# A hybrid encoder in f32: experts' steps in halves and in another order, gathers over expert 0's steps, attention scores in two row tiles

## Chip, cores and metric

One core of a Trainium2 chip. The metric is the device time of one execution, in microseconds; it is given as the median of some runs, and one further execution was recorded by the hardware profiler. Engines: PE is TensorE, PEld its weight loads, DVE VectorE, ACT ScalarE, POOL GpSimd, SP SyncE, which here only issues loads.

## What is computed

Two layers over 256 tokens of width 1024, all in f32. Cut to what matters here:

```python
for i in range(2):
    h = rms_norm(x, g_mix[i])
    q, k, v, u, gl = split(h @ w_in[i])          # q, k: 4 heads x 2 maps x 64; v: 4 heads x 128
    q, k = rope(q), rope(k)
    sc = einsum('bqhcd,bkhcd->bhcqk', q, k) * 64 ** -0.5
    pr = softmax(sc)
    a  = pr[:, :, 0] - lam * pr[:, :, 1]         # differential attention
    attn = rms_norm(einsum('bhqk,bkhe->bqhe', a, v), g_subln) @ w_attn_out[i]
    conv = silu(layer_norm(depthwise_conv(glu(u), width=31))) @ w_conv_out[i]
    x = x + (sigmoid(ga) * attn + sigmoid(gc) * conv) @ w_o[i]
    h = rms_norm(x, g_ffn[i])
    if i == 0: x = x + swiglu(h, w_ff_gu, w_ff_down)               # dense, 2816 wide
    else:      x = x + sum of the top 2 of 8 experts, each a swiglu 3584 wide
    x = x + sigmoid(rms_norm(x, g_ple[i]) @ w_ple_gate[i]) * (p[i] @ w_ple_proj[i])
return rms_norm(x, g_final)
```

An expert's weights are 1024 x 7168 and 3584 x 1024 in f32, 44 MB; the eight are 352 MB, and every one is loaded.

## The kernel before

**Dense part.** Both mixers, the dense feed-forward and the gates go through `panel` (matmuls at L298), whose weights ScalarE and VectorE first split into two parts (L272, L273). In the mixer, `scores(t)` makes for each of the 4 heads one product of 128 query tokens with both maps' 256 keys each (L426). So that one product of 128 rows makes both maps apart, the keys lie in `kTz` twice as wide: map 0's 64 rows with zeros under them, map 1's with zeros above, zeroed by POOL once per layer (L344, L345) and filled by two copies of ScalarE per 128 tokens (L409, L410). A product fills a PSUM bank of 512 columns; VectorE takes the negated maxima (L430), ScalarE the exponentials (L434). VectorE also runs most of the depthwise convolution into `acc` (L503), whose sums TensorE transposes (L191) behind the fourth gate panel. PE's order is the program's; that of the other engines is set by a scheduler.

**Experts.** The router ranks the experts by how many tokens chose them. Rank 0 is always expert 0; each rank has a fixed number of places for tokens, `SLOTS` = 64, 160, 96, 96, 96, 64, 32, 32, which is 2, 5, 3, 3, 3, 2, 1, 1 groups of 32. Tokens of a rank are gathered by a matmul (L988) into `first` (rank 0) or `xw`; `slot_scales` (L645) gathers their scales. Then an expert takes two chunks of its width, 2048 and 1536 columns of each half. For each chunk there are three steps: gate (8 loads of 1 or 0.75 MB), up (the same), down (8 or 6 loads of 1 MB). Every load is multiplied with each of the rank's groups in four column tiles of 32 (L848). After gate ScalarE applies silu out of PSUM (L874), after up VectorE multiplies (L880), before down TensorE transposes and ScalarE copies (L890, L891). After the last down step the result is scattered back to the token rows in four row tiles of 32 (L937) and added to `x` (L941); that is done in pieces beside the next expert's steps.

Two lanes, `b` with ranks 0, 6, 5, 7 and `a` with ranks 1, 2, 3, 4, are Python generators; each `next` on one writes out one step, and the loop at the end of `moe_main` decides which lane is next: `a` where the work written so far is at most `rate` times what was loaded. PE runs in that order. The gathers for ranks other than 0 are a third generator, `begin`, advanced twice after each step of expert 0; what is left of it runs before lane b's next expert.

The loads are issued by SP in the order in which TensorE uses them (`raw_block`, L255). The ring has twelve buffers of 1 MB (four `raw`, six borrowed from the dense part's weights, two in `raw2`); three more loads are made ahead into `early`. PSUM has eight banks of 512 columns for the expert part; a gate or up product takes one bank per group while it adds up, a down product one per two groups, and each bank of transposes, gather or scatter another.

Of the kernel before, what the change touches and what calls it, by code (L numbers as in the profile page):

```python
# [34 lines left out]
SLOTS = (64, 160, 96, 96, 96, 64, 32, 32)  # L35

# [14 lines left out]
def encoder_kernel(ctx: ExitStack, tc: tile.TileContext, A: dict, out: bass.AP):  # L51
# [270 lines left out]
    def mixer(i, nm, nxt, start=None, ready=(), between=None, last_hooks={}):  # L322
# [3 lines left out]
        with tc.tile_pool(name=f"mix{i}", bufs=1) as mp:  # L326
# [15 lines left out]
            with tc.tile_pool(name=f"att{i}", bufs=1) as ap, tc.tile_pool(name=f"attw{i}", bufs=2) as aw:  # L342
                kTz = ap.tile([P, NH, 2, SEQ], F32, name="kTz")
                nc.gpsimd.memset(kTz[64:128, :, 0, :], 0.0)  # L344
                nc.gpsimd.memset(kTz[0:64, :, 1, :], 0.0)  # L345
# [54 lines left out]
                def rope_T(qk):  # L400
                    for t in range(NT):
                        pt = trbank()
                        transposes([ras[qk, t][:, h * P:(h + 1) * P] for h in range(NH)], pt)
                        ptv = pt.rearrange("p (a b) -> p a b", a=NH)
                        ts = slice(t * P, (t + 1) * P)
                        if qk == 0:
                            nc.scalar.copy(qT[:, :, ts], ptv)
                        else:
                            nc.scalar.copy(kTz[0:64, :, 0, ts], ptv[0:64])  # L409
                            nc.scalar.copy(kTz[64:128, :, 1, ts], ptv[64:128])  # L410
# [12 lines left out]
                def scores(t):  # L423
                    for h in range(NH):
                        sc = bank()
                        nc.tensor.matmul(sc, qT[:, h, t * P:(t + 1) * P], kTz[:, h].rearrange("p c k -> p (c k)"),  # L426
                                         start=True, stop=True)
                        scv = sc.rearrange("p (c k) -> p c k", c=2)
                        mx = stat.tile([P, 2], F32, tag="nm", name="nm", bufs=4)
                        nc.vector.reduce_max(mx, scv, axis=AX.X, negate=True)  # L430
                        e = aw.tile([P, 2, SEQ], F32, tag="e", name="e")
                        se = stat.tile([P, 2], F32, tag="se", name="se", bufs=4)
                        for c in range(2):
                            nc.scalar.activation(e[:, c, :], scv[:, c, :], AF.Exp, bias=mx[:, c:c + 1],  # L434
# [378 lines left out]
    STEPS = [n for _, n in CHUNKS for _ in range(3)]  # L813
# [37 lines left out]
    def half_up(e, j, b):  # L851
# [4 lines left out]
        for k in range(KD):  # L856
            wt = made.pop(0) if made else raw_block(e.w_gu[:, k:k + 1, c0:c0 + n])
            e.product(ps, lambda i: e.xe[:, k, 32 * i:32 * i + 32], wt[:, 0], k == 0, k == KD - 1)
        return ps

    class Lane:


        def __init__(self, pool, name, groups):
            self.pool, self.name, self.groups = pool, name, groups
# [28 lines left out]
        def down(self, e, j, at):  # L894
# [9 lines left out]
            for l, (src, blocks) in enumerate(loads):  # L904
                wt = raw_block(src)
                for m, (g, f) in enumerate(blocks):
                    c = f * P + 32 * g
                    e.product(ps, lambda i: at[:, i, c:c + 32], wt[:, m], l + m == 0, l == len(loads) - 1 and m == 1)
            if j == 0:
# [9 lines left out]
        def scatter(self, e):  # L919
# [12 lines left out]
            for t in range(NT):  # L932
                po = [bank()[:, 0:256] for _ in range(4)]
                for i in range(e.groups):
                    for g in range(4):
                        rows = slice(32 * g, 32 * g + 32)
                        nc.tensor.matmul(po[g], selT[rows, i, t * P:(t + 1) * P], e.acc[rows, i, :], start=i == 0,  # L937
                                         stop=i == e.groups - 1, tile_position=(32 * g, 0))
                for g in range(4):
                    v = x[:, t, g * 256:(g + 1) * 256]  # L940
                    nc.vector.scalar_tensor_tensor(v, po[g], e.cmb[t], v, op0=ALU.mult, op1=ALU.add)  # L941
                yield

        def steps(self, experts, along):

# [6 lines left out]
            def beside():  # L952
                next(done, None)
                next(along, None)
                next(along, None)

            for n, make in enumerate(experts):
                if n == 1:
                    run(along)
                e = make()  # L960
                for j in range(len(CHUNKS)):
                    sil = self.silu(e, half_up(e, j, 0))
                    beside()
                    yield
                    self.times_up(e, half_up(e, j, 1), sil)
# [4 lines left out]
                    self.down(e, j, self.act_rows(e, j, sil))  # L970
# [288 lines left out]
```

## Time and profile before

| what | value |
|---|---|
| median of 3 runs | 1503.27 us (1502.98 to 1503.32) |
| the profiled execution: time, and span of its instructions | 1500.91 us, 1499.1 us |
| PE busy | 1419.3 us (95%) |
| DVE, ACT, POOL busy | 543.4, 435.1, 29.5 us |
| read from HBM | 455.41 MB, 304 GB/s over the span |
| costliest group | L848, gate and up matmuls: 453.1 us |

A busy PE is not PE at its peak: matmuls are pipelined, and ends are modelled. `A:B` in the rows is a stretch in us from the start of the span. In rows of groups the figures behind the first bar are busy time and mean ns of one, behind the second the idle time just before the group and what ended it. In rows in order of time the columns are start, length, engine, line and operation, with the idle time before in brackets. An f32 matmul of the program stands in the trace as two instructions.

### The profile page before, as it was taken

The page shows a single profiled execution, that of the slowest core. Times are in us where ns is not written, and L with a number is a line of the kernel's source. Part 1 is how long each engine was busy: PE and PEld are TensorE (multiplying, and loading weights), DVE is VectorE, ACT ScalarE, POOL GpSimd, SP SyncE. Part 2 cuts the span into 40 slices and gives each one's busy share as a digit, 9 for nine tenths or more (in the row PEclk, how much of TensorE's full clock was granted, in tenths as well). Part 3 has the DMA queues.
Part 4 walks back from the last instruction along what each step waited for, and adds up shares of the span by engine and source line. Part 5 has one row for each costly group of instructions (what it writes and reads, how often), then busy time and mean ns, then how long its engine had stood idle before and what let it go on. Part 6 is the DMA issues. An engine that isn't in the chain of part 4 may idle for free. (4 is left out here: it accounts for less than half of the span.)

```text
span 1499.1 us, 31163 instructions
## 1 busy us (share of the span) xinstructions
PE 1419.3 (95%) x13569; PEld 867.7 (58%) x13569; DVE 543.4 (36%) x1000; ACT 435.1 (29%) x748; POOL 29.5 (2%) x37
## 2 busy tenths in 40 slices
PE   8999999999999999999989999999999889899976
PEld 7777788888897777453436445244444244425346
DVE  5999665554779996100010000111010010001035
ACT  6595554443757854101000100000000000000005
POOL 2001000000000000000000000000000000000000
PEclk9999999999999999999999999999999899999998
DMA  9533655555545349897999999999999999999982
GB/s 314 186 113 113 205 183 180 186 171 177 197 168 169 111 146 370 325 368 289 407 378 419 390 397 416 421 419 419 416 417 419 421 419 418 418 419 417 410 338 85
DMA packets 116079, 458.55 MB, mean 306 GB/s; under 512 B 9590, under 2 KB 23360, under 8 KB 87264
## 3 DMA queue, kind: packets, MB, share of 16 engines
q1 hardware_dynamic: 114672, 454.69, 77.9%
q8 instruction: 108, 1.77, 0.5%
q10 hardware_dynamic: 1008, 1.65, 0.3%
q14 instruction: 35, 0.29, 0.1%
q0 software_dynamic: 256, 0.16, 0.0%
HBM read 455.41 MB, written 1.05 MB: 304 GB/s over the span
## 5 line engine op out<-in xcount | busy, mean ns | idle before, releaser
L848 PE MATMUL mm<-raw,xw 128*32 128x512 f32 (+1 forms) x4608 | 453.1, 549 | 23.5 <-DMA raw<-in_we_gu 23.4
L298 PE MATMUL mm<-w,hTb 128*128 128x512 f32 (+1 forms) x1632 | 335.3, 364 | 3.5 <-ACT hTb L218 2.9
L848 PEld LDWEIGHTS mm<-raw,xw 128*32 128x32 f32 x4608 | 149.8, 111 | 313.2 <-issue 243.0
L298 PEld LDWEIGHTS mm<-w,hTb 128*128 128x128 f32 x1632 | 275.7, 191 | 50.9 <-ACT hTb L218 3.3
L273 DVE TENSOR_TENSOR w<-raw,w 128x1024 fp32r<-128x1024 f32 (+1 forms) x196 | 228.8, 1178 | 131.5 <-ACT w L272 130.8
L848 PE MATMUL mm<-raw,aT 128*32 128x256 f32 x4480 | 248.8, 381 | 11.8 <-DMA raw<-in_we_down 8.3
L272 ACT CAST w<-raw 128x1024 fp32r<-128x1024 f32 (+1 forms) x196 | 197.8, 1017 | 207.0 <-PE mm L298 179.6
L848 PEld LDWEIGHTS mm<-raw,aT 128*32 128x32 f32 x4480 | 143.8, 110 | 111.4 <-DMA raw<-in_we_down 12.9
L880 DVE SCALAR_TENSOR_TENSOR s<-mm,rs,s 128x512 f32<-128x512 f32 (+1 forms) x40 | 27.4, 685 | 426.0 <-PE mm L848 363.3
L874 ACT ACTIVATE s<-mm,rs 128x512 f32<-128x512 f32 (+1 forms) x40 | 25.3, 634 | 333.5 <-PE mm L848 332.6
L891 ACT COPY aT<-mm 128x512 f32<-128x512 f32 (+1 forms) x40 | 19.2, 539 | 266.6 <-PE mm L890 266.5
L298 PE MATMUL mm<-w,hTa 128*128 128x512 f32 (+1 forms) x432 | 91.6, 369 | 3.4 <-DVE hTa L213 1.8
L503 DVE SCALAR_TENSOR_TENSOR acc<-zT,cw,acc 128x256 f32<-128x256 f32 x200 | 84.6, 479 | 0.1
L298 PEld LDWEIGHTS mm<-w,hTa 128*128 128x128 f32 x432 | 73.9, 188 | 18.2 <-DVE hTa L213 2.4
L298 PE MATMUL mm<-w,aTH 128*128 128x512 f32 x176 | 55.0, 391 | 0.0
L917 DVE TENSOR_TENSOR acc<-mm,acc 128x512 f32<-128x512 f32 (+1 forms) x13 | 7.0, 565 | 126.3 <-PE mm L848 126.3
L941 DVE SCALAR_TENSOR_TENSOR x<-mm,rcmb,x 128x256 f32<-128x256 f32 x64 | 26.2, 476 | 58.5 <-PE mm L937 58.5
L915 ACT COPY acc<-mm 128x512 f32<-128x512 f32 (+1 forms) x13 | 5.9, 489 | 141.2 <-PE mm L848 141.2
L185 POOL TENSOR_TENSOR rr<-rm,mhalf 128x2 f32<-128x2 f32 (+2 forms) x15 | 20.1, 1339 | 1248.2 <-DVE rm L183 1226.8
L930 DVE COPY aT<-mm 128x512 f32<-128x512 f32 (+1 forms) x13 | 7.4, 568 | 100.4 <-PE mm L191 100.4
L848 PE MATMUL mm<-raw,first 128*32 128x384 f32 (+1 forms) x464 | 43.7, 534 | 0.0
L298 PEld LDWEIGHTS mm<-w,aTH 128*128 128x128 f32 x176 | 33.0, 188 | 6.9
(239 smaller groups left out, 864.3 us busy)
## 6 DMA issues: line engine op xcount, KB each, us to landing
raw<-in_we_gu SPq DMA_DIRECT2D x125, 1024.0 KB, 19.8
raw<-in_we_down SPq DMA_DIRECT2D x112, 1024.0 KB, 19.4
raw<-in_we_gu SPq DMA_DIRECT2D x128, 768.0 KB, 14.9
raw<-in_w_in SPq DMA_DIRECT2D x35, 1024.0 KB, 4.9
raw<-in_w_ff_gu SPq DMA_DIRECT2D x22, 1024.0 KB, 5.0
raw<-in_w_ff_down SPq DMA_DIRECT2D x10, 1024.0 KB, 4.9
raw<-in_w_o SPq DMA_DIRECT2D x8, 1024.0 KB, 5.0
raw<-in_w_ple_gate SPq DMA_DIRECT2D x7, 1024.0 KB, 4.9
```

Of the source, the lines that this page charges most:

```text
L185: nc.gpsimd.tensor_tensor(r, m, mhalf[:, :count], op=ALU.pow)
L272: nc.scalar.copy(hi, src)
L273: nc.vector.tensor_tensor(lo, src, hi.bitcast(F32), op=ALU.subtract)
L298: nc.tensor.matmul(ps[t][:, :width], l, r, start=(k0 + k == 0 and j == 0), stop=(k0 + k == nk - 1 and j == 2))
L503: nc.vector.scalar_tensor_tensor(acc[:, c, :], zT[:, c, k:k + SEQ], wk[c], acc[:, c, :], op0=ALU.mult, op1=ALU.add)
L848: nc.tensor.matmul(ps[i][32 * g:32 * g + 32, :], a(i), w[:, g * q:(g + 1) * q], start=first and i % per == 0, stop=last and end, tile_posi ...
L874: nc.scalar.activation(s[:, i, 0:p.shape[1]], p, AF.Silu, scale=e.scale[:, i:i + 1])
L880: nc.vector.scalar_tensor_tensor(v, p, e.scale[:, i:i + 1], v, op0=ALU.mult, op1=ALU.mult)
L891: nc.scalar.copy(at[:, i, 0:n], pt[:, 0:n])
L917: nc.vector.tensor_tensor(d, p, d, op=ALU.add)
L930: nc.vector.tensor_copy(selT[:, i0:i0 + m, :], pt[:, 0:m * SEQ].rearrange("p (i c) -> p i c", i=m))
L941: nc.vector.scalar_tensor_tensor(v, po[g], e.cmb[t], v, op0=ALU.mult, op1=ALU.add)
```

## The change

- The scores: `kT` is as wide as `qT`, one copy per 128 tokens fills it, and there are no zeros. Two heads are taken together: four matmuls of 256 columns, each on 64 rows, write two banks, one per map, in two row tiles.
- An expert's step is divided: `half_up` and `down` yield in the middle of their loads, so a step is 4 loads (3 for the second chunk's down). The PSUM banks of a product stay taken through the yield.
- The order of the lanes follows a count, `waiting`, of loads that wait: 15 at first, and each step adds its loads times (0.36 x groups - 1), never below 0, with 0.8 more for each of the first 12 steps. Lane a is taken from step 6 on where the count after its step is at most 10. A lane that is about to begin a down product leaves the next step to the other.
- The gathers advance by one piece after each of the first half-steps, whichever lane it is.
- Lane b's scatter works with two banks at a time in place of four.

```diff
+GROUP, ROOM = 0.36, 10
@@ mixer
-                kTz = ap.tile([P, NH, 2, SEQ], F32, name="kTz")
-                nc.gpsimd.memset(kTz[64:128, :, 0, :], 0.0)
-                nc.gpsimd.memset(kTz[0:64, :, 1, :], 0.0)
+                kT = ap.tile([P, NH, SEQ], F32, name="kT")
...
-                            nc.scalar.copy(kTz[0:64, :, 0, ts], ptv[0:64])
-                            nc.scalar.copy(kTz[64:128, :, 1, ts], ptv[64:128])
+                        nc.scalar.copy((kT if qk else qT)[:, :, ts], ptv)
@@ scores
-                        nc.tensor.matmul(sc, qT[:, h, t * P:(t + 1) * P], kTz[:, h].rearrange("p c k -> p (c k)"),
-                                         start=True, stop=True)
+                        if h % 2 == 0:
+                            sc = [bank() for c in range(2)]
+                            for k in range(2):
+                                for c in range(2):
+                                    rows = slice(64 * c, 64 * c + 64)
+                                    nc.tensor.matmul(sc[c][:, k * SEQ:(k + 1) * SEQ], qT[rows, h + k, t * P:(t + 1) * P],
+                                                     kT[rows, h + k, :], start=True, stop=True, tile_position=(64 * c, 0))
...
@@ half_up, and the same in down
             e.product(ps, lambda i: e.xe[:, k, 32 * i:32 * i + 32], wt[:, 0], k == 0, k == KD - 1)
+            if k == KD // 2 - 1:
+                yield
@@ scatter
-                po = [bank()[:, 0:256] for _ in range(4)]
+                for g0 in range(0, 4, self.rows):
+                    gs = range(g0, g0 + self.rows)
+                    po = [bank()[:, 0:256] for g in gs]
@@ moe_main
-            todo = {k: [(n, n * SLOTS[i] // 32) for i in v for n in STEPS] for k, v in ranks.items()}
+            todo = {k: [(n / 2048 * 4, SLOTS[i] // 32) for i in v for n in STEPS] for k, v in ranks.items()}
+            steps, waiting, last, along = 0, 15.0, None, begin()
...
-                k = "a" if steps >= 3 and work <= rate * loaded else "b"
+                def after(k):
+                    n, groups = todo[k][0]
+                    return waiting + n * (GROUP * groups - 1)
+                k = "a" if todo["a"] and steps >= 6 and after("a") <= ROOM else "b"
...
+                waiting = max(0.0, after(k)) + (0.8 if steps < 12 else 0.0)
...
+                next(along, None)
+                if steps == 12:
+                    run(along)
```

PE, from expert 0's first down product to the first work of rank 1; `first` and `xw` are the gathered rows of expert 0 and of the others, `aT` the input of a down product, `x8` the number of matmuls. Before:

```order
L848 MATMUL mm<-raw,aT 32x256 x112
L848 MATMUL mm<-raw_5277,aT 32x256 x16
L988 MATMUL mm<-sel,ht 128x192 x32
L848 MATMUL mm<-raw,xw 32x512 x20
L848 MATMUL mm<-raw_5277,xw 32x512 x20
L848 MATMUL mm<-raw,xw 32x512 x120
L848 MATMUL mm<-raw,first 32x384 x24
```

PE, the first work of rank 1, now:

```order
L851 MATMUL mm<-raw,first 32x384 x16
L648 MATMUL mm<-tok_rstd,sel 32x1 x48
L851 MATMUL mm<-raw,xw 32x512 x80
L898 MATMUL mm<-ident,s 128x128 x6
L851 MATMUL mm<-raw,aT 32x256 x48
L851 MATMUL mm<-raw_5277,aT 32x256 x16
```

Rank 1's gate product stood behind expert 0's first chunk, 160 matmuls (8 loads) in a row; now it stands behind expert 0's second gate and up as well, 80 matmuls (4 loads), and expert 0's last down product follows before the other half.

PE, the scores of layer 0, between the value panel (`hTb`) and the transposes of the weights `a`. Before:

```order
L298 MATMUL mm<-w,hTb 128x512 x12
L426 MATMUL mm<-kTz,qT 128x512 x4
L298 MATMUL mm<-w,hTb 128x512 x48
L191 MATMUL tr<-ident,a 128x128 x8
L426 MATMUL mm<-kTz,qT 128x512 x4
```

The same place now:

```order
L300 MATMUL mm<-w,hTb 128x512 x12
L427 MATMUL mm<-kT,qT 128x256 x8
L300 MATMUL mm<-w,hTb 128x512 x48
L193 MATMUL tr<-ident,a 128x128 x8
L427 MATMUL mm<-kT,qT 128x256 x8
```

Nothing changed places; four matmuls of 512 columns became eight of 256.

PE, the end of the experts before, from the last gate and up loads of rank 4 (`xw`) on:

```order
L848 MATMUL mm<-raw,xw 32x384 x24
L890 MATMUL mm<-ident,s 128x128 x9
L848 MATMUL mm<-raw,aT 32x256 x72
L848 MATMUL mm<-raw_5277,aT 32x256 x24
...
L937 MATMUL mm<-acc,aT 128x256 x24
L890 MATMUL mm<-ident,s 128x128 x3
L848 MATMUL mm<-raw,aT 32x256 x48
L191 MATMUL mm<-ident,cols 128x128 x2
L937 MATMUL mm<-acc,aT 128x256 x8
```

The end now, from rank 4's last down loads on:

```order
L851 MATMUL mm<-raw,aT 32x256 x144
L193 MATMUL mm<-ident,cols 128x128 x6
L949 MATMUL mm<-acc,aT 128x256 x24
L851 MATMUL mm<-raw,xw 32x384 x4
...
L851 MATMUL mm<-raw,xw 32x384 x36
...
L898 MATMUL mm<-ident,s 128x128 x3
L851 MATMUL mm<-raw,aT 32x256 x48
L193 MATMUL mm<-ident,cols 128x128 x2
L949 MATMUL mm<-acc,aT 128x256 x8
```

Before, rank 7's gate and up had been done ahead of rank 4's last down product, and six down loads were left to it; now its whole second chunk, 22 loads, comes after rank 4 is done.

## Rows read from the trace of the kernel before

**Rows 1.** The page: GB/s of all loads in 40 equal slices of the span.

```profile
GB/s 314 186 113 113 205 183 180 186 171 177 197 168 169 111 146 370 325 368 289 407 378 419 390 397 416 421 419 419 416 417 419 421 419 418 418 419 417 410 338 85
```

**Rows 2.** Stretches: length, busy us of PE, PEld, DVE, ACT, POOL; clock, DMA share, GB/s.

```profile
600.00:620.00 20.00, 19.33 (x154) 8.01 (x155) 4.85 (x35) 2.86 (x4) 0.00 (x0) 0.85 0.64 241
660.00:700.00 40.00, 40.00 (x408) 13.00 (x401) 0.00 (x0) 3.44 (x5) 0.00 (x0) 1.00 0.70 248
740.00:780.00 40.00, 36.56 (x426) 14.77 (x418) 5.53 (x9) 1.55 (x3) 0.00 (x0) 1.00 0.95 370
840.00:880.00 40.00, 40.00 (x504) 16.13 (x498) 0.00 (x0) 3.49 (x6) 0.00 (x0) 1.00 0.97 377
1000.00:1020.00 20.00, 20.00 (x244) 7.77 (x240) 0.00 (x0) 0.59 (x1) 0.00 (x0) 1.00 1.01 418
```

**Rows 3.** PE in order of time, the first steps of the experts.

```profile
603.19 6.69 PE L848 MATMUL mm<-early,first 128*32 128x512 f32 x48 [0.67 <-ACT first L742]
...
618.39 2.03 PE L988 MATMUL mm<-sel,ht 128*128 128x192 f32 x16
...
636.18 1.09 PE L645 MATMUL mm<-tok_rstd,sel 128*32 128x1 f32 x96
...
638.63 14.11 PE L848 MATMUL mm<-raw,aT 128*32 128x256 f32 x256 [0.20 <-ACT aT L891]
...
656.41 34.54 PE L848 MATMUL mm<-raw,xw 128*32 128x512 f32 x320
690.77 10.50 PE L848 MATMUL mm<-raw,first 128*32 128x384 f32 x128
```

**Rows 4.** Waits of the SP queue, 660 to 700 us: in total, times, longest.

```profile
SPq L255 <- PE mm L848: 35.9, 14, 6.7
```

**Rows 5.** PE in order of time, where it waits for every load: 1 MB, then 0.75 MB.

```profile
953.99 1.92 PE L848 MATMUL mm<-raw,xw 128*32 128x512 f32 x16 [0.56 <-DMA raw<-in_we_gu]
956.49 1.92 PE L848 MATMUL mm<-raw,xw 128*32 128x512 f32 x16 [0.57 <-DMA raw<-in_we_gu]
...
1419.97 1.51 PE L848 MATMUL mm<-raw,xw 128*32 128x384 f32 x8 [0.55 <-DMA raw<-in_we_gu]
1421.85 1.51 PE L848 MATMUL mm<-raw,xw 128*32 128x384 f32 x8 [0.37 <-DMA raw<-in_we_gu]
```

**Rows 6.** Groups of the whole span: expert products, transposes, and what empties their banks.

```profile
L848 PE MATMUL mm<-raw,xw 128*32 128x512 f32 (+1 forms) x4608 | 453.1, 549 | 23.5 <-DMA raw<-in_we_gu 23.4
L848 PE MATMUL mm<-raw,aT 128*32 128x256 f32 x4480 | 248.8, 381 | 11.8 <-DMA raw<-in_we_down 8.3 <-ACT aT L891 3.5
L880 DVE SCALAR_TENSOR_TENSOR s<-mm,rs,s 128x512 f32<-128x512 f32 (+1 forms) x40 | 27.4, 685 | 426.0 <-PE mm L848 363.3 <-issue 61.1
L874 ACT ACTIVATE s<-mm,rs 128x512 f32<-128x512 f32 (+1 forms) x40 | 25.3, 634 | 333.5 <-PE mm L848 332.6
L890 PE MATMUL mm<-ident,s 128*128 128x128 f32 x140 | 21.7, 302 | 0.0
```

**Rows 7.** Groups of the whole span: scores, and the scatter in four row tiles.

```profile
L426 PE MATMUL mm<-kTz,qT 128*128 128x512 f32 x32 | 14.5, 597 | 0.0
L937 PE MATMUL mm<-acc,aT 32*128 32x256 f32 x320 | 21.1, 391 | 0.6 <-DVE aT L930 0.6
```

**Rows 8.** From the scores to the convolution's end: stretches, then PE's waits, both layers.

```profile
74.10:137.50 63.40, 58.95 (x267) 45.12 (x266) 59.80 (x134) 50.67 (x111) 5.43 (x2) 1.00 0.31 103
469.20:530.80 61.60, 58.65 (x267) 45.11 (x266) 59.13 (x132) 50.07 (x111) 3.74 (x2) 1.00 0.32 106
137.56 1.44 PE L191 MATMUL tr<-ident,acc 128*128 128x128 f32 x6 [2.44 <-DVE acc L503]
530.84 1.16 PE L191 MATMUL tr<-ident,acc 128*128 128x128 f32 x6 [1.67 <-DVE acc L503]
```

**Rows 9.** Near the experts' end: a stretch of PE, then PE's last product.

```profile
1418.00:1420.00 2.00, 1.38 (x12) 0.57 1.01 418
1453.90 1.07 PE L848 MATMUL mm<-raw,aT 128*32 128x256 f32 x16 [1.15 <-DMA raw<-in_we_down]
```

More of the change, by code (lines that the diff above doesn't have):

```diff
@@ L812, in encoder_kernel @@
     CHUNKS = ((0, 2048), (2048, 1536))
-    STEPS = [n for _, n in CHUNKS for _ in range(3)]
+    STEPS = [n for _, n in CHUNKS for _ in range(6)]
     made = []
@@ L858, in half_up, with __init__ @@
             e.product(ps, lambda i: e.xe[:, k, 32 * i:32 * i + 32], wt[:, 0], k == 0, k == KD - 1)
+            if k == KD // 2 - 1:
+                yield
         return ps
     class Lane:
-        def __init__(self, pool, name, groups):
-            self.pool, self.name, self.groups = pool, name, groups
+        def __init__(self, pool, name, groups, rows=4):
+            self.pool, self.name, self.groups, self.rows = pool, name, groups, rows
         def tile(self, kind, n=512):
@@ L908, in down @@
                     e.product(ps, lambda i: at[:, i, c:c + 32], wt[:, m], l + m == 0, l == len(loads) - 1 and m == 1)
+                if l == len(loads) // 2 - 1:
+                    yield
             if j == 0:
@@ L932, in scatter, with steps @@
             for t in range(NT):
-                po = [bank()[:, 0:256] for _ in range(4)]
[L934 to L941, printed above, removed]
+                for g0 in range(0, 4, self.rows):
+                    gs = range(g0, g0 + self.rows)
+                    po = [bank()[:, 0:256] for g in gs]
+                    for i in range(e.groups):
+                        for p, g in zip(po, gs):
+                            rows = slice(32 * g, 32 * g + 32)
+                            nc.tensor.matmul(p, selT[rows, i, t * P:(t + 1) * P], e.acc[rows, i, :], start=i == 0,
+                                             stop=i == e.groups - 1, tile_position=(32 * g, 0))
+                    for p, g in zip(po, gs):
+                        v = x[:, t, g * 256:(g + 1) * 256]
+                        nc.vector.scalar_tensor_tensor(v, p, e.cmb[t], v, op0=ALU.mult, op1=ALU.add)
                 yield
-        def steps(self, experts, along):
+        def steps(self, experts):
             done = iter(())
@@ L953, in beside @@
                 next(done, None)
[L954 to L959, printed above, removed]
+            for make in experts:
                 e = make()
                 for j in range(len(CHUNKS)):
-                    sil = self.silu(e, half_up(e, j, 0))
+                    sil = self.silu(e, (yield from half_up(e, j, 0)))
                     beside()
                     yield
-                    self.times_up(e, half_up(e, j, 1), sil)
+                    self.times_up(e, (yield from half_up(e, j, 1)), sil)
                     beside()
@@ L969, in steps @@
                         run(done)
-                    self.down(e, j, self.act_rows(e, j, sil))
+                    yield from self.down(e, j, self.act_rows(e, j, sil))
                     beside()
@@ L1107, in unit @@
                             [pc[:, t, 1:2] for t in range(NT)])
-                run(Lane(mp, "r", MORE // 32).steps([lambda: ex], iter(())))
+                run(Lane(mp, "r", MORE // 32).steps([lambda: ex]))
         def units(u):
```

26 lines of the change are left out of this document (10 added, 16 removed).

## The prediction

> **What bounds the kernel now.** I read the page first, its row of GB/s over 40 slices [rows 1]: up to about slice 14 the loads run far below what they reach later, so the dense part (both mixers, the dense feed-forward, the router) is TensorE's; from slice 24 to slice 37 they sit at 410 to 421 GB/s, so the experts, some 353 MB of weights in 368 loads, are bound by the loads there. In between, slices 15 to 23, most are short. Cut more finely, that stretch is where loads are lost [rows 2]: against the 418 GB/s of 1000 to 1020 us, the window at 600 us lacks 177 of 418 for 20 us, that is 8.5 us of loading; 660 to 700 lacks 170 for 40 us, 16.3 us; 740 to 780, 4.6 us; 840 to 880, 3.9 us. Together 33.3 us in which the load queue stood still for want of a free buffer.
>
> Why it stood still: twelve loads fit the ring, and a load is issued only when TensorE has finished with the one twelve before. The order of work on TensorE [rows 3] has a step of rank 1, which has five groups of 32 slots, from 656.41 for 34.54 us: 8 loads, 4.32 us each. A load of 1 MB takes 2.50 us and one of 0.75 MB 1.88 us where TensorE is waiting for them [rows 5]. So such a load adds 0.73 of a load to those that wait, eight of them 5.8. In those 40 us the SP queue waits 35.9 us for matmuls of L848 [rows 4]. TensorE in turn waits for loads 23.4 and 8.3 us in the whole expert part [rows 6], at other places: with few groups it is quicker than the loads. Both sides are idle by turns, which is what an order of work can mend; the bytes can't be.
>
> **Expert steps, first piece: the start.** The prices are: 34.54 us/(8 loads x 5 groups) = 0.864 us for one group of a 1 MB gate or up load; 10.50/(8 x 2) = 0.656 for a 0.75 MB one; 14.11/(8 x 2) = 0.882 for a down load [rows 3]. No arithmetic is added or removed. The first 8.5 us (600 to 620) stay: fifteen loads are in before TensorE begins at 603.19, three of them outside the ring, and nothing in the change begins earlier.
>
> Then expert 0 runs whole before rank 1, but for its last six loads, with the gathers between its half-steps. Its 40 loads cost 15.2 us for the first eight (603.19 to 618.39), 8 x 2 x 0.864 = 13.8, 14.1 for eight down loads, 16 x 2 x 0.656 = 21.0; three gathers of 2 x 2.03 + 1.09 make 15.5, and ten transposes [rows 6] 1.5: 81 us, to about 684. Loads restart near 613, so 71 us: nine of 1 MB (22.5), sixteen of 0.75 (30.1), and 18.5 us for 7.4 more. Fifteen and 32.4 have come, 40 are used: about 7 wait. The first piece of rank 1 now has 4 loads, +2.9: about 10 wait, at which point the other two are on their way. So of the 16.3 us nearly all goes; where the gathers fall late in expert 0 the ring is close to full, for which I leave 1.7 us (0 to 3).
>
> **Second piece: the middle.** Next come six loads of rank 0 and sixteen of rank 6 (one group, 0.864 us against 2.50): the ten that wait are used up, TensorE waits for loads near 725 us, and that costs nothing while the loads run. From there to the fourth half-step of rank 2 I add up: gate and up of 1 MB, 12 x 5 + 16 x 2 + 16 x 3 = 140 group-loads x 0.864 = 121 us; 0.75 MB, 16 x (5 + 1 + 2) = 128 x 0.656 = 84; down, 14 x (5 + 1 + 2) = 112 x 0.882 = 99; 56 transposes at 21.7/140 make 9 [rows 6]. Scatters of five groups are 5.3 us (21.1/20 each [rows 7]), and 4 us go to their selections and to lane b's scatter in two halves instead of four row tiles at once. That makes 322 us. The loads in it take 86 x 2.50 + 48 x 1.88 = 305 us. TensorE falls 17 us or 6.8 loads behind; the next three half-steps add 1.3. Ten may wait, so there is a margin of 1.9 loads, 5 us, and the two stalls of 4.6 and 3.9 us go too, unless something slows TensorE.
>
> That something has no row: a product cut in two keeps its PSUM banks through the other lane's step. Rank 1 holds five of eight, the other lane one or two, and the next product or transpose may wait until a bank is emptied. Emptying one takes 634 ns on ScalarE or 685 on VectorE [rows 6]. In the stretch 18 products begin. Bounds: no wait at all, or two evictions, 1.3 us, at each: 23 us, less the margin 18 us of lost loading. I take one of 0.634, 11.4 less 5: 6.4 us, since the order leaves another lane's half-step between most products and the next use of their banks.
>
> **Third piece: the end.** The last six half-steps are rank 7's alone: 22 loads with one group, bound by the loads, as the end is before. Of TensorE's clock the rows show that with 0.75 MB loads and little to do it had sunk to 0.57 of full at 1418 us, and eight instructions then take 1.51 us [rows 5, 9], where 0.656 is their full price. After the last load there are 1.07 us of matmuls [rows 9], a transpose and a scatter of about 1.2 us: at half clock at most 3 us more. I take 1.5. Once started, the part behind keeps its length.
>
> So the loads lose 8.5 + 1.7 + 6.4 = 16.6 us where they lost 33.3: 16.7 gained, less 1.5: **15.2 us**.
>
> **Scores.** Before, 16 products of 128x512 with half of the rows zero take TensorE 14.5 us [rows 7]. Now 32 of 128x256, each on half of the rows, two at a time. That row tiles do run side by side in this type is seen at L937, where 320 instructions of 391 ns each take 21.1 us, six at a time with the pipelining; those of L426 overlap 1.3 times. So 7.2 us of TensorE go, 3.6 in each layer. But VectorE has no room: from the scores to the end of the convolution it is busy 59.80 of 63.40 us in the first layer and 59.13 of 61.60 in the second [rows 8], and TensorE waits 2.44 and 1.67 us for the convolution's last sums even now. An earlier TensorE waits longer there. Only VectorE's own gaps can shrink, 3.6 + 2.5 = 6.1 us; the floor is 0, and I take the middle, **3 us**. ScalarE loses four copies and POOL four memsets, and neither is what ends last there. The maxima are as many as before, over as many elements.
>
> The Trainium skill's page "TensorEngine Tiling (Array Packing)", in Performance Considerations under PSUM Bottleneck, speaks against this edit: tiling speeds up TensorE but not the emptying of PSUM, which may then be the limit. The two VectorE rows agree that the limit is there. By that rule taken whole, this edit would give nothing, and the sum would be 1488 us.
>
> **Sum.** 15.2 + 3 = 18.2 us. The profiled execution, 1500.91 us outside of its span of 1499.1, would become 1482.7; the median of the runs is 2.4 us above the profiled one, so 1503.27 - 18.2 = **1485 us**.
>
> **Rivals.** *Banks make it slower.* If at each of the 35 half-steps of the middle TensorE waits two evictions, 46 us, less the margin 41, the loads lose 8.5 + 1.7 + 41 = 51 us against 33.3, and with the end and the scores the time is 1503.3 + 18 + 1.5 - 3 = 1520. It passes from gain to loss at 30 us of such waits, 0.85 us at each half-step. For it: five, two and one make eight banks. Against it: the two evicting engines are idle in nearly all of this part (VectorE 0.00 us busy from 660 to 700 [rows 2]), so a bank is emptied as soon as its product ends, and the scatter of lane b asks for two banks only. Chance 0.06.
>
> *The ring fills later instead.* The count starts from 15 waiting and adds for gathers; it runs rank 6 dry early, so that the heavy work is pushed behind 734 us. If TensorE's extra in the middle is 16 to 20 us and not 11.4, the stall returns near 1060 to 1100 us: 11 to 15 us lost there, 8.5 + 1.7 + 12, a gain of 11 - 1.5, and without the scores 1494 (1491 to 1500). Chance 0.18.
>
> *All of it comes.* No bank wait, no cold end, VectorE's gaps closed: 33.3 - 8.5 + 6.1 = 31 us, 1472; with some of it 1471 to 1478. Chance 0.10.
>
> *The change does nothing that counts.* The order by loads waiting moves the stalls without removing them, as the sum of work and the ring are the same: 1500 to 1506. Against it is the ledger of the start, which needs no unknown. Chance 0.06.
>
> **Numbers.** My forecast, 1478 to 1491, has 0.60. The range takes it in with about half of the better case and most of the one in which the ring fills later: 1475 to 1494. A measurement of this kernel tells 0.2%, 3 us, from no change. Faster 0.60 + 0.18 + 0.10 = 0.88, same 0.06, slower 0.06.
>
> **What would show it.** In the profile of the changed kernel: 605 to 613 us still empty of loads; 660 to 700 near 415 GB/s; TensorE waiting for loads of rank 6 near 725; the lowest later window between 1050 and 1110, at 330 GB/s or more over 40 us; the last 45 us with TensorE waiting at every load. The score products take some 7 to 8 us, and TensorE's waits for `acc` grow from 2.4 and 1.7 to 3 to 5. I am wrong if the first product of half-steps waits for ScalarE or VectorE by more than 25 us together, if windows from 740 to 1000 are short, or if the waits for `acc` do not grow.

## The result, and the profile after

The changed kernel takes 1489.62 us, the median of 6 runs (1484.58 to 1494.8), beside 1503.3 for the kernel before (1501.16 to 1507.19): the ratio, against the runs made beside it (median 1505.15), is 0.9897, 95% interval 0.9879 to 0.9914. That is 15.5 us faster (12.9 to 18.2), where 18.2 were forecast. The profiled execution took 1484.58 us with a span of 1482.8; before it was 1500.91 and 1499.1. Both lie at the fast end of their kernel's runs, 5.0 and 2.4 us under the medians.

The page's row of GB/s in 40 slices, which answers to [rows 1]:

```profile
GB/s 314 187 119 116 205 179 190 171 183 159 224 169 144 115 169 319 307 379 418 421 419 419 417 418 418 418 402 419 404 382 417 422 417 418 420 419 417 415 339 81
```

From slice 18 to 37 it stands at 415 to 422, but for slices 26, 28 and 29. Four stretches of the changed kernel, columns as in [rows 2]:

```profile
600.00:620.00 20.00, 19.32 (x148) 7.19 (x147) 3.89 (x31) 2.36 (x3) 0.00 (x0) 0.81 0.54 206
640.00:700.00 60.00, 59.57 (x902) 31.55 (x895) 2.04 (x6) 5.90 (x13) 0.00 (x0) 1.00 0.99 393
960.00:980.00 20.00, 20.00 (x323) 11.54 (x319) 0.00 (x0) 2.01 (x5) 0.00 (x0) 1.00 0.97 391
1060.00:1100.00 40.00, 40.00 (x646) 22.32 (x638) 2.83 (x7) 2.42 (x5) 0.00 (x0) 1.00 0.97 370
```

Reckoned as in the prediction, against 418 GB/s, they lose 10.1, 3.6, 1.3 and 4.6 us: 19.6 where 33.3 were lost. So 13.7 us of loading came back. The SP queue's waits from 1060 to 1100 us (in total, times, longest) show why 4.6 did not:

```profile
SPq L257 <- PE mm L851: 32.8, 18, 6.2
```

SP waits there for TensorE to free a buffer, as it did at 660 to 700 before [rows 4]. And TensorE does not wait for emptied banks. These are its waits from 738 to 1100 us:

```profile
PE mm L193 <- DVE cols L1014: 2.1, 2, 1.1
PE mm L851 <- ACT aT L899: 1.8, 4, 0.7
PE mm L851 <- DMA raw<-in_we_gu: 1.5, 2, 0.9
PE mm L949 <- DVE s L888: 0.2, 1, 0.2
```

No gate, up or down product waits for a bank. The waits for other engines are those for transposed activations, for the scatter's columns and 0.2 us of a scatter for a bank that VectorE empties: 4.1 us in 362.

At the scores, TensorE in order of time, layer 0:

```profile
74.26 2.00 PE L427 MATMUL mm<-kT,qT 64*128 64x256 f32 x16
...
109.20 1.12 PE L193 MATMUL tr<-ident,o 128*128 128x128 f32 x4 [2.42 <-ACT aT L452]
...
135.71 1.52 PE L193 MATMUL tr<-ident,acc 128*128 128x128 f32 x6 [2.49 <-DVE acc L506]
```

and the same place before:

```profile
74.12 3.67 PE L426 MATMUL mm<-kTz,qT 128*128 128x512 f32 x8
...
110.50 0.66 PE L191 MATMUL tr<-ident,o 128*128 128x128 f32 x4 [0.42 <-ACT aT L449]
```

A block of score products takes 2.00 us; before, the two blocks took 3.67 and 3.60. The wait for `acc` is what it was [rows 8]; new is 2.42 us at the transposes of `o`, for ScalarE's copy of `aT`. Before, that wait was 0.42.

### The profile page after: what moved, and what is told of

It reads as the page before. It is cut to its first block, busy times and chain, and to the rows that moved or that the text cites. A ratio compares the mean times of both kernels' runs of the same rounds, so it can differ in the third digit from the quotient of the medians.

```text
span 1482.8 us, 31201 instructions
## 1 busy us (share of the span) xinstructions
PE 1415.2 (95%) x13601; PEld 873.8 (59%) x13601; DVE 543.4 (37%) x1000; ACT 432.0 (29%) x744; POOL 23.2 (2%) x33
## 5 line engine op out<-in xcount | busy, mean ns | idle before, releaser
L851 PE MATMUL mm<-raw,xw 128*32 128x512 f32 (+1 forms) x4608 | 444.8, 543 | 16.3 <-DMA raw<-in_we_gu 16.3
L851 PE MATMUL mm<-raw,aT 128*32 128x256 f32 x4480 | 252.0, 384 | 6.8 <-ACT aT L899 3.5
L300 PEld LDWEIGHTS mm<-w,hTa 128*128 128x128 f32 x432 | 75.5, 191 | 18.2 <-DVE hTa L215 2.4
## 6 DMA issues: line engine op xcount, KB each, us to landing
raw<-in_we_gu SPq DMA_DIRECT2D x125, 1024.0 KB, 17.8
```

The lines of the kernel that those rows point to most:

```text
L300: nc.tensor.matmul(ps[t][:, :width], l, r, start=(k0 + k == 0 and j == 0), stop=(k0 + k == nk - 1 and j == 2))
L851: nc.tensor.matmul(ps[i][32 * g:32 * g + 32, :], a(i), w[:, g * q:(g + 1) * q], start=first and i % per == 0, stop=last and end, tile_posi ...
```

## Experiments

| kernel | median us | ratio to before, 95% interval |
|---|---|---|
| e1_scores: scores alone | 1505.07 | 0.9999 (0.9986 to 1.0012) |
| e2_experts: experts alone | 1490.74 | 0.9913 (0.9899 to 0.9927) |
| e3_again: the change | 1489.7 | 0.9893 (0.988 to 0.9907) |
| e4_price: other numbers in the count | 1482.07 | 0.9859 (0.984 to 0.9877) |
| e5_old_rule: halves, old order | 1501.72 | 0.9968 (0.9956 to 0.998) |
| e6_whole_steps: count, no halves | 1496.25 | 0.9927 (0.9908 to 0.9945) |
| e7_early_last | 1478.83 | 0.9822 (0.9802 to 0.9842) |
| e8_gathers_before | 1492.25 | 0.9887 (0.9856 to 0.9917) |
| e9_scores_kept_busy | 1502.94 | 0.9983 (0.9967 to 0.9999) |
| e10_best_kept_busy | 1480.45 | 0.9831 (0.9808 to 0.9855) |
| e11_early_again | 1477.15 | 0.9808 (0.9785 to 0.983) |
| e12_scores_own_bank | 1504.6 | 0.9997 (0.9984 to 1.001) |

Before was 1505.63 beside e1 to e4, 1506.12 beside e5 to e8, 1504.71 beside e9 to e11, 1505.64 beside e12.

### The two parts apart

**e1_scores** is the kernel before with only the `kT` and `scores` part of the diff; **e2_experts** is the changed kernel with the old `kTz` and `scores`.

> The kernel before with the scores in two row tiles, and nothing of the experts changed. Theory A (my forecast, the ledger of the dense part): the row tiles give 3 us of 1503.3, so 1500.3, ratio 0.998; at most 6.1, 1497.2. Theory B, from the profile of the changed kernel: the score products do take 2.00 us a block where they took 3.67, but the transposes of o now wait 2.42 us for ScalarE where they waited 0.42, and later stretches run at a lower granted clock (0.91 in 520 to 560 us), so that at the experts' start only 0.46 us of 2.9 were left: 1502.8, ratio 0.9997, same. Theory C: the lower clock comes from the scores' new wait, takes more than they give and makes the runs' times spread: 1503 to 1506, with runs more than 6 us apart. A profile in which the experts start at 600 us or earlier speaks for A, at 602.5 to 603.2 for B, later than 603.2 for C.

> The changed kernel with the mixers of the kernel before: the expert part alone. Theory A (ledger of loads): of 33.3 us that the load queue stood still, 13.7 come back and 1.4 us at the branch behind the experts, 15.1 in all: profiled 1485.8, median 1488.2, ratio 0.990. Adding e1's result gives the whole change to within 1.5 us. Theory B: the two parts help each other (an earlier start of the experts also fills the loads' ring): this one gains less than 12 us, over 1491. Theory C (the scores' new waits bring the lower clock and the spread of 10 us between the runs of the changed kernel): this one gains 17 to 18 us, 1485 to 1486, with runs within 5 us of each other.

The scores alone gain 0.2 us (-1.8 to 2.1): theory B's time, though the experts began at 605.62 us, theory C's sign; my 3 us fall. The experts alone gain 13.1 us (11.0 to 15.2), theory A, and their profiled execution was 1482.83. Runs of e2 lay 11 us apart (1482.83 to 1494.3), as far as those of the change, and those of the kernel before beside them 8 us, for 9 in e1, so the spread does not come from the scores: C falls there. The two do not quite add up: beside them the change gained 16.1 us (14.0 to 18.1, e3), 2.8 more than the two apart, where I had allowed 1.5. That is within the noise of three such measurements, so whether the scores are worth more beside the new experts stays open.

### The order, the halves and the gathers, one at a time

**e5_old_rule** puts the old rule on the new half-steps:

```diff
-k = "a" if todo["a"] and steps >= 6 and after("a") <= ROOM else "b"
+k = "a" if steps >= 6 and work <= rate * loaded else "b"
```

> The changed kernel with the old rule for the order (work done against bytes loaded, rate 1.04) on the new half-steps: divided, but not counted. Rank 1's first two half-steps then start in the middle of expert 0 and stand next to each other again. Theory A (the order by count is what regains the loads): two half-steps of rank 1 are eight loads of 4.32 us against 2.50, 5.8 more that wait, and the gathers still lie between them; 15 to 20 us are lost between 660 and 700 us and some 3 near 740, where the kernel before lost 16.3 and 4.6, and nothing at 960 to 1100: 1489.7 + 13 = 1503 (1498 to 1506), ratio to before 0.996 to 1.0. Theory B (the division alone does it, as each lane's turn is shorter): 1488 to 1493. Theory C (something in between): the stall halves, 1495 to 1498.

TensorE in e5 (in order of time), then the stretch of 640 to 700 us:

```profile
661.83 17.37 PE L851 MATMUL mm<-raw,xw 128*32 128x512 f32 x160
...
679.96 17.33 PE L851 MATMUL mm<-raw,xw 128*32 128x512 f32 x157
```

```profile
640.00:700.00 60.00, 59.46 (x844) 30.10 (x840) 3.24 (x12) 8.30 (x16) 0.00 (x0) 1.00 0.78 294
```

Rank 1's two half-steps stand together in the middle of expert 0, and 17.8 us of loads are lost again: by the ratio 4.8 us (3.0 to 6.6) are left of the gain. Halving alone is worth little; theory A.

**e6_whole_steps** keeps the count and takes the halves away:

```diff
-    STEPS = [n for _, n in CHUNKS for _ in range(6)]
+    STEPS = [n for _, n in CHUNKS for _ in range(3)]
-            if k == KD // 2 - 1:
-                yield
```

(with 8 for 4 in the count's loads, 3 for 6 in its limits, 1.6 for 0.8, and two pieces of gather per step)

> The changed kernel with undivided steps: the new count sets the order, but a step is eight loads (or seven) again, and the gathers go on two pieces at a time. Theory A: both are needed. Rank 1's first step is again 34.5 us for eight loads, 5.8 more that wait where a half adds 2.9; with about 9 waiting that is 2.5 to 3 loads over the ring, 6 to 7 us lost near 700 us; later the losses of the changed kernel (5.9 us at 960 to 1100) lie elsewhere but are of the same size: 1489.7 + 5 = 1494.5 (1492 to 1498). Theory B (the count alone does it): 1488 to 1491. Theory C (the half-steps are what frees the ring, the count adds nothing): 1500 or more.

TensorE in e6, then the stretch that it fills:

```profile
687.86 34.54 PE L851 MATMUL mm<-raw,xw 128*32 128x512 f32 x320
```

```profile
700.00:740.00 40.00, 39.72 (x470) 16.80 (x465) 0.69 (x1) 4.18 (x7) 0.00 (x0) 1.00 0.94 367
```

The whole step of 34.54 us overfills the ring: 4.9 us lost, as theory A says. So of the change's 16.1 us (e3) the count gives some 11 and the halves 5 more, which is also what the halves gave alone in e5.

**e8_gathers_before** undoes the spreading alone:

```diff
-                next(along, None)
-                if steps == 12:
+                if steps % 2 == 0:
+                    next(along, None)
+                    next(along, None)
+                if steps == 10:
                     run(along)
```

> The changed kernel with the gathers placed as in the kernel before: two pieces behind every second half-step of expert 0 and none between the others, so that the spreading alone is undone. Theory A (ledger): the same 15.5 us of TensorE before rank 1, so the number of loads that wait at 684 us is the same; a pair of pieces, 4.06 us, holds the ring 1.6 loads longer at a time, which costs only where it is full: 0 to 2 us, 1490.5 (1489 to 1492). Theory B (the spreading is what keeps 660 to 700 us filled): 5 us or more, over 1495, with 640 to 700 us below 360 GB/s.

No difference from e3 (0.9887 against 0.9893), theory A, and 640 to 700 us is as full as in the change:

```profile
640.00:700.00 60.00, 58.70 (x980) 31.83 (x984) 3.12 (x12) 7.62 (x17) 0.00 (x0) 1.00 1.00 402
```

### Where the 5.9 us in the middle went

```diff
-GROUP, ROOM = 0.36, 10
+GROUP, ROOM = 0.38, 10
-waiting = max(0.0, after(k)) + (0.8 if steps < 12 else 0.0)
+waiting = max(0.0, after(k)) + (0.4 if steps < 12 else 0.0)
```

> The changed kernel with two numbers of the count altered: a group of slots counts 0.38 of a load in place of 0.36, and the gathers 0.4 for each of the first twelve half-steps in place of 0.8. What is computed and loaded is the same; only the order of the half-steps moves. Theory A (ledger): 0.36 is short of what TensorE needs. Of one group an expert's 46 loads take it 16 x 0.864 + 16 x 0.656 + 14 x 0.882 = 36.7 us in products, and the transposes (21.7 us for 20 groups) and scatters (21.1) add 2.1; over the loads' 30 x 2.50 + 16 x 1.88 = 105.1 us that is 0.37, and what TensorE waits between them comes on top. So the count runs low, and the order lets TensorE fall behind until the ring is full at 960 and at 1060 to 1100 us (1.3 and 4.6 us of loading lost). With 0.38 these 5.9 us come back, and rank 7 ends with three half-steps alone in place of six: 1489.6 - 5.9 = 1483.7 (1480 to 1486), with 960 to 1100 us at 415 GB/s or more. Theory B (banks, not the ring, stop the loads): the order doesn't matter, 1488 to 1491. Theory C: the heavy work left for the end makes TensorE the bound there: 1490 to 1500, with windows of 1300 to 1400 us short of loads.

Three stretches of e4, and its SP queue's waits from 1060 to 1100 us:

```profile
640.00:700.00 60.00, 59.44 (x899) 31.51 (x895) 2.05 (x6) 5.91 (x13) 0.00 (x0) 1.00 1.00 397
960.00:980.00 20.00, 19.62 (x239) 8.65 (x235) 2.75 (x5) 3.17 (x7) 0.00 (x0) 1.00 1.01 417
1060.00:1100.00 40.00, 40.00 (x536) 19.34 (x532) 5.57 (x11) 1.56 (x3) 0.00 (x0) 1.00 1.01 419
```

```profile
SPq L257 <- DMA raw<-in_we_down: 16.3, 8, 2.7
SPq L257 <- DMA raw<-in_we_gu: 14.4, 7, 2.7
```

The same work in another order: both holes are closed, SP waits for the loads themselves and no longer for TensorE, and the median is 7.6 us below e3's, by the ratios 5.1. TensorE is as busy at 1060 (40.00 of 40), so a full TensorE alone does not stop the loads; a ring that is already full does. Theory A; banks (B) would not have cared about the order. The edit changes two numbers at once, so which of them moved the order is not shown. The profiled execution gained less, 2.5 us (1482.07 for 1484.58): 1.2 us are lost anew at 1200 to 1240, and the last loads come late.

### The start

**e7_early_last** is e4 with two moves: the early loads are multiplied last of the first eight, and two gathers go beside rank 6.

```diff
-        for k in range(KD):
-            wt = made.pop(0) if made else raw_block(e.w_gu[:, k:k + 1, c0:c0 + n])
+        ks = [*range(len(made), KD), *range(len(made))] if made else range(KD)
+        for at, k in enumerate(ks):
+            wt = made.pop(0) if made and at >= KD - 3 else raw_block(e.w_gu[:, k:k + 1, c0:c0 + n])
...
-                next(along, None)
-                if steps == 12:
+                if steps in (2, 4, 6, 8) or steps >= 14:
+                    next(along, None)
+                if steps == 30:
                     run(along)
```

> e4_price with two moves in the first 100 us of the experts. The three early loads, which hold no buffer of the ring, are multiplied as the last three of the first eight and not the first three; and the second and third gather stand beside rank 6, where TensorE waits for loads, and not in expert 0. Theory A (the ledger, against my own step that the first 8.5 us must stay): in e4's profile the early products take 7.87 us before the first ring buffer is used, so the load queue restarts some 7 us earlier and 10.0 us lost become 3 to 4; without 2 x (2 x 2.03 + 1.08) = 10.3 us of gathers the ring isn't full at 640 to 700 us (2.9 us lost there now). That is 9 us of loading; but TensorE waits for loads only 11.8 us from 720 to 1380 in e4, so some of it comes back as a full ring later: 5 us gained, 1477 (1472 to 1480). Theory B (TensorE's own work is the bound by now): the losses move to 1100 to 1260 us, 1481 to 1484. Theory C (the gathers wait for banks beside rank 1's five): 1485 or more, with waits of the gathers' matmuls for ScalarE or VectorE of over 5 us.

Three stretches of e7, then its first products, and those of e4:

```profile
600.00:620.00 20.00, 19.33 (x140) 8.19 (x144) 6.00 (x42) 0.58 (x1) 0.00 (x0) 0.75 0.79 309
620.00:640.00 20.00, 19.81 (x200) 7.81 (x194) 1.50 (x2) 4.58 (x7) 0.00 (x0) 1.00 0.97 379
640.00:700.00 60.00, 59.73 (x865) 34.02 (x858) 2.31 (x8) 3.73 (x8) 0.00 (x0) 1.00 1.01 415
```

```profile
604.92 11.27 PE L851 MATMUL mm<-raw,first 128*32 128x512 f32 x80 [0.67 <-ACT first L745]
616.02 5.32 PE L851 MATMUL mm<-early,first 128*32 128x512 f32 x48
```

```profile
602.36 7.87 PE L851 MATMUL mm<-early,first 128*32 128x512 f32 x48 [0.68 <-ACT first L745]
610.06 8.76 PE L851 MATMUL mm<-raw,first 128*32 128x512 f32 x80
```

Theory A, with one size off. The start loses 5.2 us up to 620 us and 1.9 more up to 640, 7.1 where e4 loses 9.8 (210 and 421 GB/s); I had expected 3 to 4. Whichever loads come first are multiplied slowly here, at a granted clock of 0.75 in the first stretch: the 80 instructions take 11.27 us first and 8.76 second, the 48 early ones 7.87 first and 5.32 second. At 640 to 700 us 0.4 is lost for e4's 3.0. The two moves are told apart by these stretches only; no run makes one of them alone. This version beats both kernels, by 26.8 us against before; **e11_early_again** is it once more.

> e7_early_last once more, beside e10 on the same chip, and for a second profile. Its time should be 1478.8 again (1476 to 1482, ratio 0.982), and if the loads and not the clock set it, the profile shows under 2.5 us lost in any window after the first 20 us of the experts, whatever the clock of the dense part was.

1477.15 us, as expected, and from 620 to 1400 us no stretch of its profile loses more than 1.4 us, at 620 to 640 us (389 GB/s); its granted clock was 0.975 to 0.982 over five runs, and the time 1473.38 to 1478.61.

### Why the scores give nothing

**e9_scores_kept_busy** and **e10_best_kept_busy** are e1 and e7 with

```diff
-                            for k in range(2):
+                            for k in (0, 1, 0, 1) if t == 1 else (0, 1):
```

> e1_scores with each score product of the second block of 128 rows made twice, the second over the first: the same result, and TensorE works 2.00 us longer in each layer. What it tests: in e1 the stretch from the first scores to the convolution's last sums is shorter (62.05 against 63.44 us in layer 0, 60.32 against 61.65 in layer 1), yet the experts start at 605.62 and not at 603.19, as TensorE waits 2.44 us for ScalarE's copy of aT and its granted clock then is 0.83 in 500 to 510 us, where the kernel before waits 0.70 and keeps 1.00. Theory A (the new wait brings the lower clock, which eats the gain): the wait shrinks to 0.4 to 0.7 us, the stretch keeps its new length since ScalarE ends it, 500 to 510 us has a clock of 1.00, the experts start at 601 to 603 us, and the time is 1502 to 1504 where before has 1505.6: ratio 0.998. Theory B (the clock has nothing to do with that wait): the dip stays, the time is that of e1 or up to 4 us more, ratio 1.000 to 1.003. Theory C (TensorE's 2.00 us are on the path after all): the stretch grows to 63.4 and 61.6, ratio 1.001 or more with no dip.

> e7_early_last with the same doubling of the score products of the second block of rows. Theory A: the wait of 2.42 to 2.52 us for aT goes to some 0.5, the clock keeps 1.00 at 500 to 510 us, and the experts start 2 us earlier than in e7 (604.92): 1476.8 against e7's 1478.8 (1475 to 1478), ratio to before 0.981. Theory B: the dip stays, 1478 to 1481. Theory C (TensorE's added 2.00 us in each layer are on the path): 1480 to 1483.

**e12_scores_own_bank** is e1 with

```diff
-                    pt = trbank()
+                    pt = trbank() if t else bank()
```

> e1_scores with one transpose of o in each layer (values_T of the first block) written to another PSUM bank, so that it no longer has to wait until ScalarE has emptied the bank with its copy of aT: the wait of 2.44 to 2.52 us is taken away by another buffer, and nothing else moves. TensorE then runs on through six products and waits for aT itself at L458 for about 0.8 us (in e1 o is ready at 501.4, the six products take 1.6 us, aT is ready at 505.3). Theory A (that wait brings the dip of the clock, 0.83 in 500 to 510 us, and the dips that follow eat the scores' gain): no dip in 495 to 535 us, the experts start at 601 to 603 us and not at 605.62, time 1501 to 1503 where before has 1505, ratio 0.997 to 0.9985. Theory B (a clock dip comes anyway, somewhere between 500 and 570 us, whatever TensorE waits for): the experts start within 604 to 606 us, ratio 0.9985 to 1.001. Theory C: the convolution's sums on VectorE end the stretch; the wait moves to acc, from 2.50 to 4 us, with or without a dip, ratio 0.998 to 1.000.

TensorE in layer 0, first in e1:

```profile
75.20 2.00 PE L425 MATMUL mm<-kT,qT 64*128 64x256 f32 x16
...
110.20 0.66 PE L191 MATMUL tr<-ident,o 128*128 128x128 f32 x4 [2.52 <-ACT aT L450]
120.38 1.10 PE L191 MATMUL tr<-ident,o 128*128 128x128 f32 x4 [0.88 <-ACT o L467]
...
137.25 1.16 PE L191 MATMUL tr<-ident,acc 128*128 128x128 f32 x6 [2.50 <-DVE acc L504]
```

then in e9:

```profile
74.18 2.00 PE L425 MATMUL mm<-kT,qT 64*128 64x256 f32 x16
88.13 3.72 PE L425 MATMUL mm<-kT,qT 64*128 64x256 f32 x32
112.74 0.66 PE L191 MATMUL tr<-ident,o 128*128 128x128 f32 x4 [4.09 <-ACT aT L450]
...
136.19 1.03 PE L191 MATMUL tr<-ident,acc 128*128 128x128 f32 x8
```

and in e12:

```profile
74.72 2.00 PE L425 MATMUL mm<-kT,qT 64*128 64x256 f32 x16
...
109.72 2.05 PE L458 MATMUL mm<-v,aT 128*128 128x128 f32 x16 [0.68 <-ACT aT L450]
119.90 1.10 PE L191 MATMUL tr<-ident,o 128*128 128x128 f32 x4 [2.65 <-ACT o L467]
...
136.76 1.16 PE L191 MATMUL tr<-ident,acc 128*128 128x128 f32 x6 [2.49 <-DVE acc L504]
```

Both of my ways to remove the wait failed to. In e9 the wait grew to 4.09 us, as the second block's scores come later and ScalarE with them; in e12 it moved behind `o`. From the first scores to the end of the convolution's transposes it is 63.21 us in e1 (75.20 to 138.41), 63.04 in e9, which has 1.72 us more of TensorE, and 63.20 in e12; before it was 64.88. So of the 3.3 us that the products save, 1.7 come. TensorE's speed is not what ends the stretch any more: the rest it waits, now for ScalarE's `aT`, now for `o`, now for `acc`. By its time and by the experts' start, 604.78 us, e12 is theory B. e9 has theory A's time, 2.6 us (0.2 to 5.0) below before, but not by its way: the wait grew, and the granted clock falls all the same (0.84 from 510 to 520 us).

In layer 1 1.3 us come, 61.48 against 62.81. These are its ends in e1, with the experts' start, and its first scores before:

```profile
469.86 2.00 PE L425 MATMUL mm<-kT,qT 64*128 64x256 f32 x16
...
530.18 1.16 PE L191 MATMUL tr<-ident,acc 128*128 128x128 f32 x6 [1.44 <-DVE acc L504]
...
605.62 8.03 PE L849 MATMUL mm<-early,first 128*32 128x512 f32 x48 [0.68 <-ACT first L743]
```

```profile
469.19 3.67 PE L426 MATMUL mm<-kTz,qT 128*128 128x512 f32 x8
```

The two stretches together give 3.0 us, and more than that is lost before the experts begin, at 605.62 us in e1 for 603.19: the first scores come 1.1 us later, 1.3 us go between the stretches, and 3.1 behind layer 1's sums (74.28 us to the experts for 71.19). There TensorE waits in e1 for VectorE's `pT`, and from 590 us runs slower:

```profile
580.51 0.66 PE L191 MATMUL tr<-ident,x 128*128 128x128 f32 x4 [1.22 <-DVE pT L609]
...
590.69 2.09 PE L686 MATMUL mm<-wrs,hTb 128*128 128x16 f32 x9 [0.24 <-DVE hTb L219]
592.63 5.21 PE L298 MATMUL mm<-w,pT 128*128 128x512 f32 x12
...
599.28 5.66 PE L741 MATMUL mm<-sel,ht 128*128 128x64 f32 x32
```

Before, these three took 1.17, 4.57 and 5.33 us and `pT` was not waited for: 1.22 + 0.92 + 0.64 + 0.33 make 3.1 us.

The other profiles have it too. In the ten with the quicker scores and no doubled products the stretches take 62.69 to 63.75 and 61.43 to 62.08 us, and the part behind them 73.39 to 74.28; in the two with the old scores it is 64.88 and 65.16, 62.81 and 62.77, and then 71.19 and 71.96. e9 and e10, with the doubled products, need 71.48 and 69.28 us for the part behind; both have a granted clock of 0.83 from 590 to 600 us, where e1 has 0.66 and the kernel before 0.78. So a longer part behind goes with a lower clock; what brings it is not shown, and e10's runs were not faster than e11's (1480.45 against 1477.15). A part of these differences may also lie between executions: the two profiles with the old scores are 2.4 and 7.9 us under their kernels' medians, that of e1 is at its own.

### A second profile of the change

> The changed kernel once more, for a second profile beside the others on the same chip. Its first runs lay between 1484.6 and 1494.8 us with mean granted clocks from 0.975 to 0.967, lower where the time is longer. Theory A: the difference between runs is the clock in the dense part (before 600 us) and behind the experts; the windows from 620 to 1400 us, counted from the experts' start, load within 1 us of the same. Theory B: it is the clock in the middle of the experts, where TensorE has no idle time (40.00 of 40 us busy in 1060 to 1100): there a lower clock turns into lost loads, and a slower profile shows windows of 960 to 1100 us with 3 us or more lost than the 5.9 of the first profile. Median 1489.6 (1485 to 1494), ratio 0.990.

Its median is that of the first runs. Its profiled execution took 1492.96 us, 8.4 more than the first. Two stretches of it:

```profile
703.00:763.00 60.00, 53.15 (x502) 18.39 (x498) 4.37 (x9) 1.55 (x3) 0.00 (x0) 0.86 1.01 421
980.00:1060.00 80.00, 77.58 (x952) 31.86 (x948) 6.71 (x18) 4.08 (x7) 0.00 (x0) 0.98 1.00 405
```

The granted clock from 703 to 763 us is 0.86, where the first profile has 0.94. The loads do not suffer there (421), but 980 to 1060 us, filled in the first profile, then has 405 GB/s, 2.5 us lost. The experts began 3.9 us later (606.59 against 602.73), and from there to the end it took 4.5 us longer. Neither theory holds as written: the experts' loads do differ, against A, but 960 to 1100 us loses 7.8 us for 5.9, and B asked for 3 us more.

## Why the prediction was right, and where a step failed

**Start, first piece.** 8.5 us were to stay; 10.1 did. That nothing could begin earlier was true of this change; e7, which uses the early loads last, loses 7.1 us there, so some 3 us of it can go. Late in expert 0 I left 1.7 us, and it is 3.6 (3.0 in e4, 0.4 in e7, where two gathers are gone from there): the ring is full beside the gathers, as said, only longer.

**Middle.** 6.4 us were taken, 5.9 came, but not for my reason: that the sizes agree is luck. I priced 18 bank evictions of 0.634 us; there are no such waits. What I missed is the order itself: the count prices a group at 0.36 of a load, and with 0.38, and half the price for the gathers, the loss is gone (e4). I had added up TensorE's work against the loads to one point, rank 2's fourth half-step, and called the margin of 5 us enough for the rest; the rival in which the ring fills later had the place right, 1060 to 1100 us, and the loss there was 4.6 and not 11 to 15.

**End.** 1.5 us for a cold TensorE; these three rows of the changed kernel took 1.93, 0.69 and 2.09 us, where before they took 1.07, 0.44 and 1.15, so 2.05:

```profile
1436.24 1.93 PE L851 MATMUL mm<-raw,aT 128*32 128x256 f32 x16 [0.57 <-DMA raw<-in_we_down]
1438.10 0.69 PE L193 MATMUL mm<-ident,cols 128*128 128x128 f32 x2
1439.38 2.09 PE L949 MATMUL mm<-acc,aT 32*128 32x256 f32 x16 [0.58 <-DVE aT L940]
```

No term had the wait at the branch behind the experts, 4.86 us for 6.24. The experts' 15.2 us measured 13.1 (11.0 to 15.2): my figure is the upper end of the interval.

**Scores.** This step failed: 3 us taken, 0.2 (-1.8 to 2.1) measured. What I had worked out from VectorE's gaps came: in e1 the two stretches are 1.67 and 1.33 us shorter, 3.0 together, though I took the middle of 0 to 6.1 with no row for it. What failed is a step that I did not write down, that the rest of the kernel keeps its length: in e1 it is 5.4 us longer up to the experts' start, 3.1 of it behind layer 1's sums. The cause of that is open. The place of the wait was wrong too: the waits for `acc` did not grow (2.49 and 1.68 us), which I had named as a sign of being wrong; the first new wait is for a bank that ScalarE empties. The Trainium skill's rule is that tiling speeds up TensorE and not the emptying of PSUM ("TensorEngine Tiling (Array Packing)", Performance Considerations, PSUM Bottleneck). The trace agrees in part: 2.42 us of waiting for ScalarE's copy out of PSUM are new, yet the stretch did become shorter. By that rule taken whole the sum was 1488, nearer to 1489.6 than mine.

**Signs.** TensorE waits for rank 6's loads from 723 to 738 us, 740 to 960 us is filled, the lowest later window is 370 GB/s at 1060 to 1100, and the score products take four times 2.00 us, all as forecast; 660 to 700 us has 404 GB/s, where I said near 415.

## What to carry to other kernels

Where two streams of work share a ring of loads, order them by a count of what waits, and price a unit of work with all that comes with it (transposes, scatters, waits): other prices, 0.38 of a load for 0.36 and 0.4 for 0.8, were 5 us here. A buffer outside the ring should be used after those in it: at the start of the experts some 3 us here. A quicker product is worth what is left of it at the end: two stretches became 3.0 us shorter and the kernel 0.2 us (-1.8 to 2.1) faster. Before counting it, find which wait takes over, and whether the part behind keeps its length.

## What was unexpected

The granted clock. In rows of 10 us, all twelve profiles with the quicker scores have it at 0.88 or less somewhere between 500 and 570 us, in the second layer, and in neither of the two with the old ones. One such stretch of e1 and the same of the kernel before:

```profile
500.00:510.00 10.00, 7.56 (x36) 6.22 (x35) 9.57 (x22) 8.71 (x16) 0.22 (x1) 0.83 0.11 40
```

```profile
500.00:510.00 10.00, 9.30 (x56) 7.84 (x55) 9.18 (x20) 9.44 (x21) 0.44 (x1) 1.00 0.20 76
```

0.83 is a mean of the two levels, 1.2 and 2.4 GHz: in e1 the clock is 1.00 up to 505 us, the end of TensorE's wait for `aT`, and 0.50 from 506 to 508. TensorE is 7.56 us busy where it was 9.30. That the longer wait brings the fall fits e9 and e12, in which it comes at 510 to 520 us, behind the moved wait. Against it speak the change's first profile, e4 and e11: the rows from 500 to 520 us stay at 1.00 behind the same wait of 2.42 to 2.45 us, and the fall comes between 520 and 570. No kernel here removed the waiting, so the cause stays open. And a low clock need not cost where it occurs: in e3 no loads are lost from 703 to 763 us, and those lost come more than 200 us later, where TensorE is 77.58 of 80 us busy. That the one brings the other is not shown.
